# Two standard merge tiles fewer beside the first branch, one more pair by seven products, in an encoder trunk on Trainium2

## The chip, the cores and the metric

The kernel runs on one core of one Trainium2 chip. Its engines are TensorE (PE: matmuls, with PEld for weight loads), VectorE (DVE), ScalarE (ACT), GpSimd (POOL, hardly used here) and SyncE (SP, which only issues transfers here). ScalarE issues transfers too, from the same queue as its arithmetic (ACTq in the rows). The metric is device microseconds of one execution, the median of several runs.

## The reference

One layer of an encoder over 16 meta tokens, 512 prompt tokens and 256 sample tokens, with 2048 features, in float32. Normalised inputs are projected once, three mixers work on parts of the result, and sigmoid gates merge them:

```python
h = rmsnorm(z, norm_g)
cols = h @ w_in
u_a, gate_a, q_b, k_b, v_b, gate_b, glr_b, x_c, gate_c, merge = split_cols(cols)
y_a = s5_mixer(u_a, ...) * jax.nn.silu(gate_a)
y_b = gla_mixer(q_b, k_b, v_b, glr_b, ...) * jax.nn.silu(gate_b)
y_c = rglru_mixer(x_c, ...) * jax.nn.silu(gate_c)
gates = jax.nn.sigmoid(merge).reshape(bsz, length, N_BRANCH, D_MODEL)
m = (gates[:, :, 0] * (y_a @ w_out_a) + gates[:, :, 1] * (y_b @ w_out_b)
     + gates[:, :, 2] * (y_c @ w_out_c))
return z + m @ w_o
```

The `merge` part has 3 x 2048 columns: 48 tiles of 128 columns, each needed only near the end, when the branches are merged. They can be computed at any time after the input is normalised.

## The kernel before, in words

Each float32 product is made of three products of split halves (high x high, high x low, low x high), so one 128x128 weight block times 768 tokens is 6 matmuls of 384 columns.

**Two ways to a merge tile.** A standard tile (`merge_tile`, `fill_step`) goes over 16 blocks of features: 16 steps of 6 matmuls, 96 in all. The rest of the tiles are made in pairs in `strassen`, by seven products of half size in place of eight (`products`, `combine`): 168 matmuls for a pair. `NST` is the number of merge pairs made that way; 48 - 2 `NST` tiles are standard. With `NST` = 15 there are 18 standard tiles. Two are computed while the inputs are normalised, the other 16 are in the list `merges`. Every tile, made either way, is copied and spilled to memory (`gspill`).

**Standard tiles as cover.** The first branch (`branch_s5`) is mostly VectorE work with long chains. So that TensorE has something to do beside it, steps of standard tiles are put between its pieces. `Paced` wraps VectorE and adds up a charge for every operation. At each `tick` (line 287) a step (`fill_step`, matmuls at line 273) is written into the program for as long as the sum of charges is ahead of the steps' own clock, which advances by 1 / rate a step. The rate is the entry of `FILLS` for the stage, set by `pace`: 0 for the parameters, 1 for the chunk inputs, 2 for the scan over chunks (`advance`), 3 for the chunk outputs, 4 for gelu. Before stage 5 (the gating product, matmuls at line 728), and at each later call, `pace` also calls `flush`, which finishes an open tile. Stages 5 to 7 have rate 0. What is left in `merges` goes beside the end of the third branch (`cover(LT)`, 39 steps) and beside the first sums of `strassen`.

**The stages that the change touches.** In stage 3, for eight chunks e: `within(e + 2)` prepares coefficients (VectorE operations on `ca`, in three buffers; small products at line 634; `kt` copies on ScalarE; the store `kd` and the four loads `tp` on ScalarE's queue), then `chunk_out(e)` does 12 matmuls (lines 652 to 654), copies into `W`, and after chunks 3 and 7 stores `yd`. Stage 4 loads `fu` and `fy` on ScalarE's queue and computes gelu of four blocks (`fz`, `fh`, `fl`); stage 5 multiplies them by the gating weights. Then `branch_gla` begins: keys and queries are projected (matmuls at line 199, into the same four banks `psA` that the standard tiles use, two for each) and copied to `kk` and `qq`, then the values.

**What sets the order.** A planner at build time orders each engine's instructions: at each point the earliest in the program that it holds to be ready by its own costs. On the chip every engine then runs its list in that order. So work written later can stand earlier in an engine's list, and an instruction that waits holds up all behind it.

Of the kernel before, what the change touches and what calls it, by code (L numbers as in the profile page):

```python
# [19 lines left out]
HT = T // 2  # L20
HN = NT // 2
MAGIC = 12582912.0
FILLS = (0.2, 0.7, 1.6, 0.8, 1.1, 0, 0, 0)
SCRATCH = 1024
AHEAD = 6
SPLITN = 12
NST = 15
NA = 3
PREP = 6
WH = 3  # L30
# [65 lines left out]
def build(tc, A, out_p, out_s):  # L96
# [134 lines left out]

    merges = list(enumerate(MERGES[:48 - 2 * NST]))
    def merge_tile():
        i, (d, b) = merges.pop(0)
        merge_out(proj(MERGE0 + i, NM), d, b)
# [57 lines left out]
    def flush():  # L293

        fill["last"] = True
        while fill["k"] < 16 or fill["ws"]:
            fill_step()
        fill["last"] = False
# [86 lines left out]
    def pace(i):  # L385
        if i > 4:
            flush()
        fill.update(rate=FILLS[i], us=V.us)

# [1170 lines left out]
def strassen(E):  # L1560
# [52 lines left out]
    def weights(i, sb):  # L1613
        r = wp.tile([128, 4, 2, 128], F32, name="raw", bufs=2)
        SP.dma_start(r[:], A["w_st"][i, sb])
        rh = wp.tile([128, 3, 2, 128], F32R, name="hi")
        rl = wp.tile([128, 3, 2, 128], F32R, name="lo")
        split(rh[:], rl[:], r[:, 1:4])
        t = tp.tile([128, 4, 2, 128], F32, name="t")
        weight_sums(V, r, t)  # L1620
        th = wp.tile([128, 4, 2, 128], F32R, name="hi")
        tl = wp.tile([128, 4, 2, 128], F32R, name="lo")
        split(th[:], tl[:], t[:])
        return rh, rl, th, tl
# [14 lines left out]
    xp = tc.alloc_tile_pool(name="stu", bufs=1, reuse_waits="tile")  # L1639
    for i in range(NG2 + NST):  # L1640
        ps = {j: next_bank() for j in (1, 2, 3, 6, 7, 5, 4)}
        for sb in range(4):
            products(PE, ps, ahead.pop(0), sb, 8, operand)
            n = 4 * i + sb + 1
            if n > 2 and n < 4 * (NG2 + NST):
                ahead.append(weights(*divmod(n, 4)))
# [6 lines left out]
        if i < NG2:  # L1653
# [9 lines left out]
            continue  # L1663
        for g, (d, b) in zip((g1, g2), MERGES[48 - 2 * NST + 2 * (i - NG2):]):
            S.dma_start(E["gspill"][d, :, b, :], g[:])
# [29 lines left out]
def layout(inp):  # L1695
# [7 lines left out]
    order = [36 + 16 * b + d for d, b in MERGES]  # L1703
    std = order[:48 - 2 * NST]
    D["w_in"] = np.ascontiguousarray(w3[[i for i in range(36) if i not in GATES] + std])
    pairs = GATES + order[48 - 2 * NST:]
    st = []
# [88 lines left out]
```

## Time and profile before

| | us |
|---|---|
| median of three runs | 2037.04 |
| lowest and highest | 2035.94, 2038.36 |
| the profiled execution | 2038.42 |
| its span, first to last instruction | 2036.6 |

TensorE's granted clock was 0.996 of the full one in the mean. Engine idle time is read together with what ended it: an engine that is not the bottleneck may idle at no cost.

### The profile page before, as it was taken

The numbers are of one execution on the slowest core, as the hardware profiler recorded it, in microseconds if no ns is written. First come the engines' busy times: TensorE is split into PE (matmuls) and PEld (weight loads), VectorE is DVE, ScalarE is ACT, GpSimd is POOL, SyncE is SP. The second block draws the span as 40 slices with busy tenths as digits, with TensorE's granted clock in tenths as the row PEclk, the third lists the DMA queues.
The fourth block names the chain that finished last, engine by engine and source line by source line (L and its number), as shares of the span: only waits on it lengthen the run. The fifth ranks groups of instructions, "written<-read, shape, count | busy, mean of one in ns | idle before, by whom it ended". The sixth has DMA issues, their size and how long they took to land.

```text
span 2036.6 us, 30982 instructions
## 1 busy us (share of the span) xinstructions
PE 2003.8 (98%) x12228; PEld 1972.5 (97%) x12228; DVE 1504.9 (74%) x2784; ACT 808.2 (40%) x1172; POOL 0.2 (0%) x4
## 2 busy tenths in 40 slices
PE   8999999999999999999999999999999999999997
PEld 8999999999989999999999999999999999999997
DVE  8988983656567876977676656665669989887778
ACT  7332111443437675433333222222235435533345
POOL 0000000000000000000000000000000000000000
PEclk9999999999999999999999999999999999999999
DMA  8762234421111323543443222322355335532256
GB/s 292 251 123 94 75 102 120 147 80 49 61 52 45 102 72 122 179 133 102 139 135 112 94 94 100 103 91 100 104 183 215 125 114 180 176 117 94 94 163 218
DMA packets 105378, 252.12 MB, mean 124 GB/s; under 512 B 18960, under 2 KB 39952, under 8 KB 105232
## 3 DMA queue, kind: packets, MB, share of 16 engines
q1 hardware_dynamic: 77072, 200.61, 30.8%
q10 hardware_dynamic: 28160, 49.53, 6.9%
q8 instruction: 96, 1.57, 0.3%
q14 instruction: 50, 0.41, 0.1%
HBM read 200.65 MB, written 49.45 MB: 123 GB/s over the span
## 4 chain that ended last, share of the span: by engine, by line
PE 78%; DVE 13%; ACT 4%; DMA 3%; issue 1%; ACTq 0%; SPq 0%; DVEq 0%
PE pm L1149 24%; PE br L1149 23%; PE pm L199 10%; PE pm L273 5%; PE br L1422 4%; PE pm L1292 2%; PE br L1292 2%; DVE sc L61 2%; DVE W L61 2%; PE pm L332 2%; DVE lo L61 2%; ACT gt L89 1%; DMA c<-gspill 1%; DVE hb L61 1%; PE br L199 1%
## 5 line engine op out<-in xcount | busy, mean ns | idle before, releaser
L89 ACT ACTIVATE hi<-raw 128x768 fp32r<-128x768 f32 (+2 forms) x234 | 216.1, 924 | 482.8 <-PE br L1149 129.0
L61 DVE TENSOR_TENSOR lo<-raw,hi 128x768 fp32r<-128x768 f32 (+2 forms) x234 | 246.3, 1053 | 131.5 <-ACT hi L89 131.1
L61 DVE TENSOR_TENSOR lo<-t,hi 128x1024 fp32r<-128x1024 f32 x140 | 171.5, 1225 | 193.4 <-ACT hi L89 193.2
L89 ACT ACTIVATE hi<-t 128x1024 fp32r<-128x1024 f32 x140 | 148.4, 1060 | 279.6 <-PE pm L1149 138.3
L1149 PE MATMUL pm<-l,hi 128*128 128x384 f32 (+1 forms) x616 | 197.3, 320 | 0.0
L1149 PE MATMUL pm<-h,hi 128*128 128x384 f32 (+1 forms) x616 | 196.6, 319 | 0.2 <-ACT g L89 0.2
L1149 PE MATMUL pm<-h,lo 128*128 128x384 f32 (+1 forms) x616 | 196.6, 319 | 0.0
L1149 PE MATMUL br<-l,hi 128*128 128x384 f32 (+1 forms) x504 | 167.1, 331 | 0.0
L1149 PE MATMUL br<-h,hi 128*128 128x384 f32 (+1 forms) x504 | 165.9, 329 | 0.0
L1149 PE MATMUL br<-h,lo 128*128 128x384 f32 (+1 forms) x504 | 165.8, 329 | 0.0
L199 PE MATMUL pm<-h,hi 128*128 128x392 f32 (+1 forms) x608 | 161.8, 344 | 1.2 <-ACT xp L1022 1.2
L199 PE MATMUL pm<-h,lo 128*128 128x392 f32 (+1 forms) x608 | 159.5, 342 | 1.0 <-DVE lo L61 1.0
L199 PE MATMUL pm<-l,hi 128*128 128x392 f32 (+1 forms) x608 | 159.6, 341 | 0.0
L273 PE MATMUL pm<-h,lo 128*128 128x384 f32 x512 | 131.6, 338 | 2.5 <-DVE lo L61 2.5
L273 PE MATMUL pm<-h,hi 128*128 128x384 f32 x512 | 133.8, 342 | 0.0
L273 PE MATMUL pm<-l,hi 128*128 128x384 f32 x512 | 132.6, 340 | 0.0
L1149 PEld LDWEIGHTS pm<-h,hi 128*128 128x128 f32 x616 | 115.7, 188 | 0.7 <-ACT g L89 0.5
L1149 PEld LDWEIGHTS pm<-h,lo 128*128 128x128 f32 x616 | 116.0, 188 | 0.0
L1149 PEld LDWEIGHTS pm<-l,hi 128*128 128x128 f32 x616 | 115.7, 188 | 0.0
L199 PEld LDWEIGHTS pm<-h,hi 128*128 128x128 f32 x608 | 111.0, 188 | 2.7 <-ACT xp L1022 1.5
L199 PEld LDWEIGHTS pm<-h,lo 128*128 128x128 f32 x608 | 111.2, 188 | 1.5 <-DVE lo L61 1.3
L199 PEld LDWEIGHTS pm<-l,hi 128*128 128x128 f32 x608 | 110.6, 188 | 0.2
(358 smaller groups left out, 4799.6 us busy)
## 6 DMA issues: line engine op xcount, KB each, us to landing
raw<-in_w_st SPq DMA_DIRECT2D x92, 512.0 KB
raw<-in_w_in SPq DMA_DIRECT2D x74, 512.0 KB
gspill<-g ACTq DMA_DIRECT2D x48, 384.0 KB
raw<-in_w_ost SPq DMA_DIRECT2D x32, 512.0 KB
xr<-in_xT SPq DMA_DIRECT2D x31, 392.0 KB
m<-gspill SPq DMA_DIRECT2D x26, 384.0 KB
raw<-in_w_out SPq DMA_DIRECT2D x16, 512.0 KB
raw<-in_w_outc SPq DMA_DIRECT2D x16, 512.0 KB
```

Of the source, the lines that this page charges most:

```text
L61: return f(*a, **k)
L89: ins = self.eng.activation(**k)
L199: PE.matmul(ps[h][:, :nw], w[:, k, :], xx[kt][:, n0 + h * nw:n0 + (h + 1) * nw], start=(kt == 0 and j == 0), stop=(kt == 15 and j == 2))
L273: PE.matmul(ps[h][:, :HN], w[:, k % 8, :], xx[k][:, NM + h * HN:NM + (h + 1) * HN], start=(k == 0 and j == 0), stop=(k == 15 and j == 2))
L332: PE.matmul(ps0[2 * t + h][:, :HT], w[:, k, :], xx[kt][:, h * HT:(h + 1) * HT], start=(kt == 0 and j == 0), stop=(kt == 15 and j == 2))
L1149: PE.matmul(ps[j][:, :nt], w[:, wi, kk, :], x, start=(k == 0 and q == 0), stop=(k == n - 1 and q == 2))
L1292: PE.matmul(ps[h][:, :HN], w[:, 4 * b + k, :], yy[4 * b + k][:, h * HN:(h + 1) * HN], start=(k == 0 and j == 0), stop=(k == 3 and j == 2))
L1422: PE.matmul(po[:, :NS], x[:, n, :], y[k][:, ss], start=(first and j == 0), stop=(last and j == 2))
```

## The change

```diff
-FILLS = (0.2, 0.7, 1.6, 0.8, 1.1, 0, 0, 0)
+FILLS = (0.2, 0.7, 1.6, 0.15, 0.85, 0, 0, 0)
-NST = 15
+NST = 16
```

One more pair of merge tiles is made by seven products, so two fewer are standard; the rates of standard steps beside the chunk outputs (stage 3) and gelu (stage 4) are lower. The layout of the weights follows from `NST`; nothing else is edited.

## Rows read from the trace of the kernel before

**Rows 1.** The page's table of engines: busy us (share of the span), instructions.

```profile
PE 2003.8 (98%) x12228; PEld 1972.5 (97%) x12228; DVE 1504.9 (74%) x2784; ACT 808.2 (40%) x1172; POOL 0.2 (0%) x4
```

**Rows 2.** Busy time by stretch; the columns are in the first line.

```profile
core 0: us, PE busy (x) PEld busy (x) DVE busy (x) ACT busy (x) POOL busy (x), PEclk, DMA share, GB/s
285.00:382.00 97.00, 97.00 (x687) 93.78 (x686) 48.60 (x125) 21.44 (x42) 0.00 (x0) 1.00 0.47 143
382.00:415.00 33.00, 30.87 (x173) 29.51 (x172) 22.85 (x23) 15.84 (x23) 0.00 (x0) 1.00 0.41 130
415.00:456.00 41.00, 41.00 (x225) 39.80 (x224) 23.46 (x47) 15.67 (x29) 0.00 (x0) 1.00 0.19 65
900.00:1500.00 600.00, 600.00 (x3438) 600.00 (x3438) 393.06 (x602) 180.34 (x216) 0.00 (x0) 1.00 0.33 110
```

**Rows 3.** Groups of instructions: matmuls of standard steps (one of three groups).

```profile
L273 PE MATMUL pm<-h,lo 128*128 128x384 f32 x512 | 131.6, 338 | 2.5 <-DVE lo L61 2.5
```

**Rows 4.** Timeline of TensorE: start, length, line, tiles, count [idle before].

```profile
285.42 0.66 PE L634 MATMUL br<-ca,b 128*32 128x128 f32 x16
...
324.65 0.67 PE L634 MATMUL br<-ca,b 128*32 128x128 f32 x16
...
327.95 0.60 PE L273 MATMUL pm<-h,hi 128*128 128x384 f32 x2
...
342.73 0.35 PE L652 MATMUL br<-U,tp 128*128 128x96 f32 x2
...
381.76 0.52 PE L199 MATMUL pm<-h,lo 128*128 128x392 f32 x2
382.12 0.86 PE L728 MATMUL br<-fh,fwh 128*128 128x384 f32 x4
```

**Rows 5.** Timeline of ScalarE and its queue, 326 to 415 us.

```profile
326.25 2.47 ACTq L644 DMA_DIRECT2D tp<-kd  x4
...
342.76 0.49 ACT L89 ACTIVATE g<-pm 128x384 f32<-128x384 f32 x1 [12.08 <-PE pm L273]
342.94 0.60 ACTq L644 DMA_DIRECT2D tp<-kd  x1
...
364.92 0.87 ACT L89 ACTIVATE g<-pm 128x384 f32<-128x384 f32 x2 [14.08 <-PE pm L273]
...
366.69 0.48 ACTq L697 DMA_DIRECT2D fy<-yd  x1
...
414.78 0.89 ACT L89 ACTIVATE kk<-pm 128x392 f32<-128x392 f32 x2 [0.86 <-DVE fy L61]
```

**Rows 6.** Waits, 285 to 430 us: total, times, longest.

```profile
ACT g L89 <- PE pm L273: 26.2, 2, 14.1
...
DVE ca L61 <- PE br L653: 3.7, 3, 2.0
```

**Rows 7.** Timeline of ScalarE: copies of the first product, first and last of 23.

```profile
867.18 0.48 ACT L1163 COPY u<-br 128x384 f32<-128x384 f32 x1 [0.33 <-PE br L1149]
...
1512.61 0.46 ACT L1163 COPY u<-pm 128x384 f32<-128x384 f32 x1
```

**Rows 8.** TensorE around two idle places, and the clock by stretch.

```profile
268.94 0.62 PE L273 MATMUL pm<-h,lo 128*128 128x384 f32 x2 [2.04 <-DVE lo L61]
...
759.90 1.01 PE L1053 MATMUL br<-xch,gwh 128*128 128x402 f32 x4 [1.92 <-ACT xch L89]
...
269.40:272.80 3.40, 3.40 (x13) 3.40 (x13) 3.25 (x16) 0.65 (x1) 0.00 (x0) 0.53 0.42 154
273.00:276.40 3.40, 3.40 (x21) 3.40 (x21) 3.20 (x16) 0.97 (x3) 0.00 (x0) 1.00 0.29 116
761.00:764.00 3.00, 3.00 (x11) 2.97 (x10) 0.00 (x0) 1.82 (x4) 0.00 (x0) 0.52 0.00 0
```

**Rows 9.** Timeline of TensorE: end of the queries, end of the values.

```profile
418.47 0.51 PE L199 MATMUL pm<-h,lo 128*128 128x384 f32 x2
...
455.80 0.27 PE L822 MATMUL br<-ident,tmp 128*16 128x128 f32 x1
```

## Prediction

> **What bounds the kernel now.** I read the page's engine table first: TensorE is busy 98% of the span, VectorE 74%, ScalarE 40% [rows 1]. So time is TensorE work plus what TensorE waits. Then the table by stretch, for the stretches that the edit touches and the one where the added pair will lie: TensorE is full from 285 to 382 us, loses 2.1 us between 382 and 415, and is full again to 456 and over 900 to 1500 [rows 2]. VectorE is busy 49 of the 97 us up to 382. The order on TensorE comes next [rows 3, 4], then ScalarE's queue and its waits [rows 5, 6]: these tell how much later the first branch's own chain runs than it has to, because standard tile steps stand ahead of it.
>
> **What changes in the order.** One step of a standard tile is 6 matmuls, a tile 16 steps; the trace has 512 matmuls of each of the three operand kinds at L273, thus 1536 or 16 tiles [rows 3]. I count steps with the helper's own charges (0.065 us and 0.00104 us a column), which fix the order and are no times. A chunk's `within` is charged 5.0 us, six of them 30.0; at rate 0.8 this gives 25 steps (from the first tick on, so one more than the product), at 0.15 it gives 5. Gelu is charged 15.8: 18 steps at 1.1, 14 at 0.85. `flush` ends the open tile. Up to there 122 steps are unchanged, so before: 122 + 25 + 18 + 11 of the flush = 176 = 11 tiles; after: 122 + 5 + 14 + 3 = 144 = 9 tiles. With 14 tiles to place instead of 16, five are left for the third branch and the Strassen sums in both kernels, so nothing is moved there. The edit takes 32 steps away: 20 beside the chunk outputs, 12 beside gelu and its flush.
>
> **The part removed.** In the Strassen loop there are 23 copies of a pair's first product, the first at 867.18 and the last at 1512.61 us [rows 7]: 22 distances of 29.34 us, for 168 matmuls, 174.6 ns each. A standard step's matmuls keep that pace: 14 steps, 84 matmuls, fill the 14.78 us from 327.95 to 342.73 [rows 4], 176 ns each. Two tiles are 192 x 174.6 ns = **33.5 us** of TensorE. With them go four 512 KB loads on SP's queue and four splits (1.06 us on ScalarE and 1.22 us on VectorE each), which lie beside other work.
>
> **The part added.** One pair more: **29.3 us**, in a loop where TensorE is busy 600.00 of 600 us [rows 2]. Its four loads are of the same size and go on the same queue; its two spills replace the two tiles' spills on ScalarE's queue. VectorE has 393 us of work in 600 there [rows 2], about 19 us per 29.3, so its new splits and sums are covered; without cover it would be those 19 us. I put nothing on top.
> The Trainium skill, "TensorE: Matmul & The Clock Gate", section "Back-to-back issue gap", gives N/2.4 + 2.5 ns, for 384 columns an estimate of 162.5 ns. By it the tiles are 31.2, the pair 27.3 and the difference 3.9 us instead of 4.2. The measured pace decides.
>
> **What of the 33.5 us comes off the path.** If TensorE stayed full, all of it: 33.5 - 29.3 = 4.2 us faster. But where tiles were cover, their going shows the chain beneath. I follow it to the copy of the keys (`kk`) at 414.78 us, after which TensorE has its value projections to do up to 455.80 whatever came before [rows 5, 9]. The terms:
> - ScalarE stood 12.08 and 14.08 us in front of copies `g<-pm`, each waiting for the last step of a standard tile; behind the first stood the load of the last chunk's block (`tp`, 342.94), behind the second the loads that begin gelu (`fy`, 366.69) [rows 5]. That is 26.2 us in which the chain was merely queued [rows 6]. Fewer steps ahead of it give these back: 26.2.
> - The chunk loop: five rounds from 285.42 to 324.65, 7.85 us each [rows 4]. In a round VectorE builds `ca` anew once a chunk output has freed its buffer, and the next small products need it. VectorE waited 3.7 us for chunk outputs [rows 6]: all of it is given back if outputs run as soon as they can, nothing if the loop holds its order. Neither row is nearer, so the middle: 1.9.
> - Queries: their last matmul began at about 418.6, 4 us after `kk` could be copied [rows 5, 9]. With work pulled ahead they are done by then: 4.0, and 0 if not.
> - Against it: of a round's 7.85 us TensorE's own small products and chunk output take 3.3 (324.65 to 327.95 [rows 4]) and the one step left about 1.05, so it must find 3.5 us elsewhere. The planner does pull work forward: keys run at L199 ahead of the first matmul at L728, and 13 steps written for gelu ran between two chunk outputs [rows 4]. Where it fails there is a gap. After gaps of 2.04 and 1.92 us the granted clock was 0.53 and 0.52 in the stretch behind, the 1.2 GHz level. There 13 matmuls began in 3.4 us, at the full level 21: 8 x 0.175 = 1.4 us a time [rows 8]. I take one such drop; bounds 0 and five.
> The same page, in its section "Why this matters for your kernels", says that idle gaps throttle the array. The rows agree, and it speaks against thinning the cover.
>
> Sum: 26.2 + 1.9 + 4.0 - 1.4 = 30.7 us saved, 29.3 added: **1.4 us faster**. The profiled execution took 2038.42 (span 2036.6 and 1.8 around), so 2037.0 by it; it lies 1.38 above the median of the three runs, 2037.04. On the median's scale: **2035.6 us**.
>
> **Rivals.**
> - *Full cover.* The planner fills every gap with the 17 steps left, keys and queries. For it: they run ahead already, 16.8 us each. Against: four banks hold two projections, and no third can start before `kk` is copied. Time: 2037.04 - 4.2 = 2032.8; if the two idle places of 382 to 415 close too, 2030.8.
> - *Slower: the wrong place in the queue.* TensorE and ScalarE run in the planner's order. The `tp` loads of the seventh chunk were issued by 328.7, yet its output began at 342.73, behind a run of 14 steps [rows 4, 5]. If the planner puts 14 steps there again (the 17, or keys), the first 12.08 us are not given back, and these steps are then missing as cover beside gelu, where TensorE idles. Saved 30.7 - 12.1 = 18.6, net 10.7 slower: 2047.7; if half of it stays, 2041.7. It decides from less than 29.3 us saved.
> - *Slower: the clock.* Every round of the chunk loop leaves a gap long enough for the drop: four more at 1.4 us, 5.6 - 1.4 = 4.2 slower, 2041.2. Against: the small products keep TensorE occupied through much of a round, and the pulled work.
>
> **Chances.** Forecast (2033 to 2039.5) 0.50; full cover 0.26; wrong place 0.15; clock 0.09. A measurement of this kernel tells about 0.2%, 4.07 us, from no change. Full cover is just beyond it: faster 0.26. The forecast lies within it, with part of the clock's case: same 0.51. The rest is slower: 0.23. The range goes from the better end of full cover, 2031.0, to between the two sizes of the wrong place, 2043.5. The tail above holds about 0.1, the one below less.
>
> **What would show it.** Strassen copies still 29.3 us apart, the groups at L273 smaller by 64 (448). The `kk` copy between 384 and 392 us: at 389.5 or so the change breaks even, for 25.3 us earlier with the queries done (4.0) is 29.3. Waits of `g<-pm` for TensorE down from 26.2 to a few us. TensorE idle between 285 and 415 up by 2 to 5 us. Wrong if the seventh chunk output still stands behind a run of steps while gelu starts late, if the clock falls in several rounds, or if five tiles are not what is left.

## The result, and the profile after

The changed kernel took **2051.36 us** (median of 6 runs, 2050.20 to 2053.45), the kernel before 2037.13 on the same chip: ratio 1.007, 95% interval 1.0057 to 1.0083. It is 14.2 us slower, where I had forecast 1.4 faster and a range that ended at 2043.5. The profiled execution took 2050.43 (span 2048.0).

The engine table and the table by stretch of after, for the stretches of [rows 1, 2], and one of the three groups of standard steps [rows 3]:

```profile
PE 2004.7 (98%) x12204; PEld 1969.6 (96%) x12204; DVE 1515.1 (74%) x2807; ACT 808.6 (39%) x1173; POOL 0.2 (0%) x4
...
core 0: us, PE busy (x) PEld busy (x) DVE busy (x) ACT busy (x) POOL busy (x), PEclk, DMA share, GB/s
285.00:382.00 97.00, 92.05 (x622) 86.98 (x621) 57.64 (x136) 25.62 (x43) 0.00 (x0) 0.97 0.49 149
382.00:415.00 33.00, 27.04 (x130) 24.58 (x129) 20.61 (x36) 16.42 (x29) 0.00 (x0) 0.93 0.16 57
415.00:456.00 41.00, 40.85 (x232) 38.24 (x231) 21.99 (x50) 12.95 (x29) 0.00 (x0) 1.00 0.15 52
900.00:1500.00 600.00, 600.00 (x3438) 600.00 (x3437) 386.25 (x588) 177.16 (x208) 0.00 (x0) 1.00 0.32 106
...
L273 PE MATMUL pm<-h,lo 128*128 128x384 f32 x448 | 115.2, 338 | 4.1 <-DVE lo L61 4.1
```

TensorE does less (12204 matmuls for 12228), yet is busy 0.9 us longer: part of its work ran at half clock. Between 285 and 456 us it was idle 11.1 us, before 2.1. The Strassen loop is as full as before.

ScalarE's copies of a pair's first product, first and last of now 24 [rows 7]:

```profile
848.62 0.48 ACT L1163 COPY u<-br 128x384 f32<-128x384 f32 x1 [0.33 <-PE br L1149]
...
1523.38 0.46 ACT L1163 COPY u<-br 128x384 f32<-128x384 f32 x1
```

23 distances of 29.34 us. The loop begins 18.6 us earlier (of which 17.0 are there at the end of the values) and ends 10.8 us later: 18.6 gained, 29.3 paid. So the question is what became of the 33.5 us that two tiles cost. TensorE's timeline of after at the places of [rows 4, 8, 9]:

```profile
321.84 0.42 PE L273 MATMUL pm<-h,hi 128*128 128x384 f32 x1
...
330.15 0.51 PE L199 MATMUL pm<-h,hi 128*128 128x392 f32 x2
...
338.72 0.35 PE L652 MATMUL br<-U,tp 128*128 128x96 f32 x2
...
369.45 0.86 PE L728 MATMUL br<-fh,fwh 128*128 128x384 f32 x4
...
377.86 1.65 PE L728 MATMUL br<-fh,fwh 128*128 128x384 f32 x4 [3.53 <-ACT fh L89]
...
386.46 0.44 PE L728 MATMUL br<-fh,fwh 128*128 128x384 f32 x1 [1.44 <-ACT fwh L89]
...
388.76 0.44 PE L728 MATMUL br<-fh,fwl 128*128 128x384 f32 x1 [1.34 <-DVE fwl L61]
...
399.85 0.83 PE L199 MATMUL pm<-h,hi 128*128 128x392 f32 x2 [3.18 <-ACT kk L89]
...
438.80 0.27 PE L822 MATMUL br<-ident,tmp 128*16 128x128 f32 x1
```

First, 47 matmuls of standard steps (from 321.84) and 48 of a projection (330.15 to 338.72) stand between the sixth chunk's output and the seventh's, 16.9 us without a pause, where 14 steps had stood for 14.8 us. Then the rest of keys and queries runs, all of it before the gating matmuls begin at 369.45. From there TensorE has nothing but gating to do, and stops four times. ScalarE and its queue in the same stretch [rows 5]:

```profile
310.83 2.48 ACTq L644 DMA_DIRECT2D tp<-kd  x4
313.35 6.14 ACTq L660 DMA_DIRECT2D yd<-W  x7
319.54 0.27 ACT L637 COPY kt<-br 128x128 f32<-128x128 f32 x1 [12.43 <-DMA yd<-W]
...
330.17 0.49 ACT L89 ACTIVATE g<-pm 128x384 f32<-128x384 f32 x1 [7.60 <-PE pm L273]
330.41 0.60 ACTq L644 DMA_DIRECT2D tp<-kd  x1
...
331.05 4.36 ACTq L644 DMA_DIRECT2D tp<-kd  x7
...
352.89 0.44 ACTq L697 DMA_DIRECT2D fy<-yd  x1
...
383.89 1.99 ACT L89 ACTIVATE ft<-br,small 128x384 f32<-128x384 f32 x4 [2.64 <-PE br L728]
...
399.30 0.89 ACT L89 ACTIVATE kk<-pm 128x392 f32<-128x392 f32 x2 [0.71 <-DVE fy L61]
```

and the waits of after, 285 to 430 us [rows 6] (total, times, longest):

```profile
ACT kt L637 <- DMA yd<-W: 12.4, 1, 12.4
ACT kt L637 <- DMA tp<-kd: 10.7, 2, 6.1
...
ACT g L89 <- PE pm L273: 7.6, 1, 7.6
```

The hold for standard tiles is down from 26.2 to 7.6, as forecast. But the 7.6 that are left stand in front of the `tp` loads of the seventh and of the last chunk (issued from 330.41 to 335.41), where the 12.08 of before stood in front of the last one's alone. And another hold has grown: the copy `kt` for the seventh chunk stands behind eight stores of chunk outputs to `yd` (L660) that ScalarE issues itself. The last seven take it 0.88 us each here, and the copy starts 0.05 us after them. The trace of before had that wait too, in a row that I did not use:

```profile
317.52 4.11 ACTq L660 DMA_DIRECT2D yd<-W  x7
321.67 0.27 ACT L637 COPY kt<-br 128x128 f32<-128x128 f32 x1 [8.71 <-DMA yd<-W]
```

**Where the 33.5 us went.** Of these, 17.0 arrived at L822. Additional idle time from 285 to 456 us is 8.9. Two stretches after stops ran at the half level of the clock (first and third row; columns as in the table by stretch):

```profile
376.60:383.40 6.80, 5.54 (x16) 5.02 (x17) 4.63 (x6) 2.85 (x4) 0.00 (x0) 0.50 0.32 96
384.00:387.00 3.00, 1.56 (x9) 1.24 (x9) 2.02 (x2) 2.41 (x5) 0.00 (x0) 1.00 0.00 0
400.50:403.90 3.40, 3.40 (x11) 3.08 (x11) 2.42 (x5) 0.45 (x2) 0.00 (x0) 0.51 0.07 26
```

At granted clocks of 0.50 and 0.51, 5.54 and 3.40 us of work lost 4.4 us. A stop of 2.0 us from 277.5 (a `lo` split on VectorE), where before stopped for 0.46, adds 1.5. 17.0 + 8.9 + 4.4 + 1.5 = 31.8; 1.7 us I can't assign.

### The profile page after: what moved, and what is told of

Read it like the earlier page. It is cut to its first block, busy times and chain, and to the rows that moved or that the text cites. A ratio compares the mean times of both kernels' runs of the same rounds, so it can differ in the third digit from the quotient of the medians.

```text
span 2048.0 us, 30986 instructions
## 1 busy us (share of the span) xinstructions
PE 2004.7 (98%) x12204; PEld 1969.6 (96%) x12204; DVE 1515.1 (74%) x2807; ACT 808.6 (39%) x1173; POOL 0.2 (0%) x4
## 4 chain that ended last, share of the span: by engine, by line
PE 78%; DVE 13%; ACT 4%; DMA 4%; issue 1%; ACTq 0%; SPq 0%; DVEq 0%
PE br L1149 24%; PE pm L1149 23%; PE pm L199 10%; PE pm L273 3%; PE pm L1422 3%; PE br L1292 2%; PE pm L1292 2%; DVE sc L61 2%; DVE W L61 2%; DVE lo L61 2%; PE pm L332 2%; PE br L1422 1%; DMA x<-xnorm 1%; ACT gt L89 1%; DVE hb L61 1%
## 5 line engine op out<-in xcount | busy, mean ns | idle before, releaser
L1149 PE MATMUL br<-l,hi 128*128 128x384 f32 (+1 forms) x576 | 187.6, 326 | 0.0
L1149 PE MATMUL pm<-l,hi 128*128 128x384 f32 (+1 forms) x576 | 187.5, 326 | 0.0
L1149 PE MATMUL br<-h,lo 128*128 128x384 f32 (+1 forms) x576 | 186.7, 324 | 0.1
L1149 PE MATMUL pm<-h,lo 128*128 128x384 f32 (+1 forms) x576 | 186.6, 324 | 0.0
L1149 PE MATMUL br<-h,hi 128*128 128x384 f32 (+1 forms) x576 | 186.4, 324 | 0.0
L273 PE MATMUL pm<-h,lo 128*128 128x384 f32 x448 | 115.2, 338 | 4.1 <-DVE lo L61 4.1
L273 PE MATMUL pm<-h,hi 128*128 128x384 f32 x448 | 117.2, 342 | 0.0
L273 PE MATMUL pm<-l,hi 128*128 128x384 f32 x448 | 116.1, 340 | 0.0
L199 PEld LDWEIGHTS pm<-l,hi 128*128 128x128 f32 x608 | 111.0, 188 | 0.2
L1149 PEld LDWEIGHTS br<-h,lo 128*128 128x128 f32 x576 | 108.5, 188 | 0.4 <-DVE lo L61 0.4
```

The costliest lines, as they stand in the source:

```text
L199: PE.matmul(ps[h][:, :nw], w[:, k, :], xx[kt][:, n0 + h * nw:n0 + (h + 1) * nw], start=(kt == 0 and j == 0), stop=(kt == 15 and j == 2))
L273: PE.matmul(ps[h][:, :HN], w[:, k % 8, :], xx[k][:, NM + h * HN:NM + (h + 1) * HN], start=(k == 0 and j == 0), stop=(k == 15 and j == 2))
L1149: PE.matmul(ps[j][:, :nt], w[:, wi, kk, :], x, start=(k == 0 and q == 0), stop=(k == n - 1 and q == 2))
```

## Experiments

Three theories. **The list**: the chain of the first branch is held by ScalarE's own list: the `yd` stores stand in front of the work of the last chunks, and taking standard steps away leaves that hold. **Cover**: the lower rates are at fault (too few steps as cover, and with them the clock), whatever the queues do. **Price**: the pair itself costs more than 29.3 us. (Where an expectation below says "theory A" or "rival", it spells out beside it which one it means in that run.) Marks, in us, of all kernels (the sixth and the last chunk: start of the last matmul of its output; the ratio is to the kernel before as it was measured beside each):

| kernel | sixth chunk | last chunk | `kk` copy | first L822 | first L1163 copy | time | ratio (95%) |
|---|---|---|---|---|---|---|---|
| before | 327.9 | 350.0 | 414.8 | 455.8 | 867.2 | 2037.1 | 1 |
| after | 321.8 | 343.9 | 399.3 | 438.8 | 848.6 | 2051.4 | 1.0057–1.0083 |
| e1 rates alone | 325.6 | 347.8 | 403.4 | 442.8 | 884.7 | 2054.0 | 1.0065–1.0095 |
| e2 pair alone | 327.0 | 349.2 | 413.4 | 454.4 | 855.4 | 2058.5 | 1.0089–1.0119 |
| e3 after, 16 stores on SyncE | 319.4 | 330.2 | 390.1 | 431.0 | 842.0 | 2046.4 | 1.0027–1.0055 |
| e4 before, same | 327.5 | 335.1 | 418.7 | 471.7 | 881.2 | 2057.2 | 1.0079–1.0109 |
| e5 after, 8 stores on SyncE | 319.5 | 330.2 | 392.2 | 431.7 | 840.9 | 2046.5 | 1.0033–1.006 |
| e6 before, same | 327.4 | 335.5 | 401.5 | 454.5 | 864.3 | 2037.0 | 0.9987–1.0005 |
| e7 more cover beside chunks | 326.3 | 349.5 | 411.3 | 450.8 | 857.4 | 2058.3 | one run |
| e8 cover beside gelu only | 320.9 | 344.8 | 399.8 | 439.2 | 849.6 | 2054.4 | one run |
| e9 = e5 + held queries | 319.7 | 330.7 | 390.4 | 428.0 | 838.2 | 2040.9 | 1.0003–1.0021 |
| e10 after + held queries | 325.0 | 347.1 | 402.0 | 439.6 | 850.3 | 2051.7 | 1.0053–1.008 |
| e11 pair, lower `LT` | 327.2 | 349.4 | 413.9 | 454.9 | 859.5 | 2060.7 | 1.01–1.0127 |

The marks are those of the one profiled execution of each, the times are medians. In e5 and e3 that execution was the shortest (2041.39 and 2043.44). And up to the sixth chunk e1 and e10 have the work of after, yet reach it at 325.6 and 325.0 and not at 321.8: in both TensorE's clock was at 0.50 for over 6 us in the chunk loop. So single marks differ by up to 4 us for that reason alone.

### The two halves of the change

e1 is the kernel before with the rates of after:

```diff
-FILLS = (0.2, 0.7, 1.6, 0.8, 1.1, 0, 0, 0)
+FILLS = (0.2, 0.7, 1.6, 0.15, 0.85, 0, 0, 0)
```

> The lower rates alone, still 15 pairs: nine standard tiles beside the first branch, and the two that are left over go beside the third branch's end and the Strassen sums. If the first branch gave back only 17.0 of the 33.5 us in the changed kernel because its own chain is bare there, and TensorE is full where the two tiles go, the time is 2037.1 + 16.5 = 2053.6 us. Rival: the sums are short of cover and take the tiles for less than their 33.5 us: 2040 to 2048.

e2 is the kernel before with the pair alone:

```diff
-NST = 15
+NST = 16
```

> One pair more at the old rates: the first branch keeps eleven tiles, so two fewer are left for the third branch's end and the Strassen sums (three instead of five). If the pair's price is 29.3 us and those places need no cover, 2037.1 - 4.2 = 2032.9 us. If the sums are a chain of their own that the tiles cover (41 steps before, 9 here), up to all of the 33.5 us stays: 2037 to 2066. The keys' copy stands at 414.8 us as in the kernel before, by either.

e1 took 2053.99 us, 16.0 more than the kernel before beside it (2037.97) and as expected (2053.6), though it computes the very same tiles in the same way: they are only placed later, some 20 steps of them after 840 us, ahead of the Strassen loop. So the loss comes from the place, and the price theory falls: the loss is there without the pair, and the pair costs 29.34 us in the loop. (The medians of e1 and after lie 2.6 us apart, which their intervals don't tell from nothing.) With the old rates the pair makes it worse still, 2058.47, inside the second range of its expectation. TensorE's timeline of e2, at its largest stop:

```profile
832.12 0.69 PE L1149 MATMUL br<-sh,hi 128*128 128x384 f32 x1 [24.00 <-ACT hi L89]
```

The two tiles are then missing beside the sums of the Strassen operands: TensorE waits 24.0 us for ScalarE, and from 832 to 836 us, behind the stop, the granted clock is 0.50. So the standard steps are cover in both places. That fits the count in the prediction: with five tiles left for the third branch and the sums, that part of after is as full as before's.

e11 tries whether the third branch can spare them (fewer steps there, so that more are left for the sums):

```diff
-LT = 39
+LT = 15
```

> The kernel before with the one pair more (NST 16) and its own rates, and the charge of steps beside the third branch's last part lowered from 39 to 15, so that the sums of the Strassen loop's operands keep 33 standard steps beside them instead of 9. The run e2_pair_alone had lost 24.0 us of TensorE there. Theory A (the two tiles can be missed beside the third branch but not beside the sums): the 24 us gap at 808 us is gone, the stretch up to 458 us is as in before, time 2033 to 2037. Rival (the steps were cover beside the third branch too): TensorE idles there by about as much as it gains, time 2045 to 2060.

TensorE of e11, three of its stops:

```profile
787.67 1.01 PE L273 MATMUL pm<-h,hi 128*128 128x384 f32 x2 [2.99 <-ACT hi L89]
...
793.56 1.01 PE L273 MATMUL pm<-h,lo 128*128 128x384 f32 x2 [4.24 <-DVE lo L61]
...
835.60 0.69 PE L1149 MATMUL br<-sh,hi 128*128 128x384 f32 x1 [14.36 <-ACT hi L89]
```

It took 2060.68 us: the expectation of theory A is missed. The time is 0.7 us above the rival's range, but not by its mechanism: the third branch's own matmuls show no new stop; the one in the sums went from 24.0 to 14.4 us, and TensorE waited 7.2 us for the weights of standard steps at 787 and 793 us. The lower charge moved only two steps before 770 us. Whether the third branch can spare a tile stays open.

### How many steps, and where

e7 puts the steps beside the chunk outputs (`FILLS` 0.7 and 0 there and beside gelu), e8 beside gelu only (0 and 0.85), both with the pair:

```diff
-FILLS = (0.2, 0.7, 1.6, 0.15, 0.85, 0, 0, 0)
+FILLS = (0.2, 0.7, 1.6, 0.7, 0, 0, 0, 0)     # e7
+FILLS = (0.2, 0.7, 1.6, 0, 0.85, 0, 0, 0)    # e8
```

> The changed kernel with the same nine standard tiles, but all 22 steps left placed beside the chunk outputs (rates 0.7 and 0). If the chain of the first branch sets the time, the keys' copy stands within 4 us of the changed kernel's 399.3, whatever place the steps have. If it is the place of the cover, more of it beside the chunk outputs holds the last chunk back, the keys' copy comes at 403 or later: 2055 us or more.

> The same nine tiles with no step beside the chunk outputs and 22 beside gelu and its flush (rates 0 and 0.85). Chain: the keys' copy within 4 us of 399.3, 2047 to 2055 us. Place of the cover: fewer steps in front of the last chunks, the keys' copy at 395 or earlier, 2046 us or less.

e8 had `kk` at the same place as after (399.8), within the range of its first expectation. Its last chunk still comes 23.9 us behind the sixth, in before and after 22.1. ScalarE and TensorE in e8:

```profile
312.48 4.15 ACTq L660 DMA_DIRECT2D yd<-W  x7
316.67 0.27 ACT L637 COPY kt<-br 128x128 f32<-128x128 f32 x1 [9.34 <-DMA yd<-W]
...
322.48 5.00 ACTq L644 DMA_DIRECT2D tp<-kd  x8
```

```profile
331.01 0.51 PE L199 MATMUL pm<-h,hi 128*128 128x392 f32 x2
...
339.59 0.36 PE L652 MATMUL br<-U,tp 128*128 128x96 f32 x2
```

The hold at the stores is there again, but it is not what the seventh chunk waits for last: all eight `tp` loads are issued by 327.5, and two chunks earlier an output began 2.1 us after its loads were issued. The seventh output begins at 339.59, behind 57 matmuls of steps and 48 of a projection that run without a pause. No step is charged to the chunk outputs here; the planner pulled steps written for gelu into the place, and keys behind them. So in e8 TensorE's order holds the last chunks.

e7 had `kk` 12.0 us later than after, as its second expectation said, but it is no test of the place alone: its trace has 160 steps ahead of the third branch, ten tiles and not the nine that were expected, so it carries one tile (16.8 us of matmuls) more there. With 64 steps left where after has 80, TensorE stopped 11.7 us in the sums. Each of the two has one time only, so the marks are what is read here.

### The stores on ScalarE's queue

e3 is the kernel after, e4 the kernel before, with all 16 stores of the last two blocks issued by SyncE:

```diff
-                S.dma_start(ydv[j, :, gs], W[j * 16:(j + 1) * 16, gs, 97:193])
+                SP.dma_start(ydv[j, :, gs], W[j * 16:(j + 1) * 16, gs, 97:193])
```

> The changed kernel with the sixteen stores of the chunk outputs (yd) issued from SyncE's queue and not from ScalarE's. Theory A (ScalarE's queue: its stores, loads and waiting copies stand in the first branch's chain, 12.4 us of them in front of the seventh chunk's kt copy): the last chunk output ends 6 to 12 us earlier, the keys' copy too, and the time falls to 2039 to 2045 us. Theory B (the chain is long by latencies and by gelu itself, wherever its transfers are issued): the keys' copy moves by under 3 us, 2048 to 2052 us.

> The kernel before with the same stores on SyncE's queue. Both theories: TensorE is full there, so within 2 us of 2037.1 us. A gain of over 4 us would say that the kernel before is held by that queue too.

In e3 the last chunk follows the sixth by 10.8 us instead of 22.1, and L822 comes 7.8 us earlier than in after: that speaks for the list. The time, 2046.38, is 1.4 us above theory A's range. SyncE's queue also carries loads. ScalarE in e3, and SyncE's queue and TensorE in e4:

```profile
349.01 0.63 ACT L89 ACTIVATE fwh<-fw 128x512 fp32r<-128x512 f32 x1 [12.40 <-DMA fw<-in_w_glu]
```

```profile
313.44 38.79 SPq L660 DMA_DIRECT2D yd<-W  x16
```

```profile
379.52 1.33 PE L728 MATMUL br<-fh,fwh 128*128 128x384 f32 x3 [14.87 <-ACT fh L89]
```

In e4 the stores occupy that queue for 38.8 us (the last eight follow the last chunk's output), and the weight loads behind them are issued only from 352 us on. TensorE's list has no projection between the standard steps and gating there, and it stops for 14.9 us until gelu's first results (`fh`). I had expected no change from e4 and it lost 0.94%: a miss. It fits the list theory on another queue; how much of the stop is the queue and how much the planner's order is not separated.

So e5 (after) and e6 (before) move only the eight stores of the first of the two blocks:

```diff
-                S.dma_start(ydv[j, :, gs], W[j * 16:(j + 1) * 16, gs, 97:193])
+                (SP if e == 3 else S).dma_start(ydv[j, :, gs], W[j * 16:(j + 1) * 16, gs, 97:193])
```

> The changed kernel with only the first eight stores of the chunk outputs (after the fourth chunk) on SyncE's queue; the last eight stay on ScalarE's. Theory A (those eight issues stand in front of the seventh chunk's kt copy, and the sixteen on SyncE held up the loads of the gating weights): the last chunk output ends near 330 us as with all sixteen moved, gelu's first square comes before 345 (349.6 there), the keys' copy stands at 383 to 387, under the 389.5 us at which the change breaks even, and the time is 2031 to 2036 us. Theory B (gelu and the gating product are long by themselves): the keys' copy stays at 390 or later and the time is 2042 to 2047 us.

> The kernel before with the same eight stores on SyncE's queue. TensorE is full there in either theory: within 3 us of 2037.5 us, if SyncE's loads of the standard tiles' weights are not held up by them; 2050 or more if they are, as with all sixteen.

ScalarE in e5:

```profile
314.54 0.27 ACT L637 COPY kt<-br 128x128 f32<-128x128 f32 x1 [2.09 <-DMA tp<-kd]
...
320.63 0.27 ACT L637 COPY kt<-br 128x128 f32<-128x128 f32 x1 [5.68 <-DMA tp<-kd]
...
363.22 1.06 ACT L89 ACTIVATE hi<-raw 128x1024 fp32r<-128x1024 f32 x1 [4.31 <-DMA raw<-in_w_in]
...
376.79 1.99 ACT L89 ACTIVATE ft<-br,small 128x384 f32<-128x384 f32 x4 [6.17 <-PE br L728]
```

The wait for stores is gone, sixth to last chunk is 10.7 us, and e5 is 4.9 us faster than after. But the edit changed more than that wait. TensorE at the seventh output of e5:

```profile
321.99 0.36 PE L652 MATMUL br<-U,tp 128*128 128x96 f32 x2
```

Only 9 matmuls of steps stand between the sixth and this one, where after has 47 and 48 of a projection: with the stores elsewhere the planner made another order. So e5 and e3 show that the place of the eight stores decides when the last two chunks come. They don't tell the wait on the chip from the planner's order, and e8 speaks for the order.

The numbers miss: I expected 2031 to 2036 and got 2046.49. 24.1 us saved at L822 are 5.2 less than 29.3, which accounts for the profiled execution (2041.39) and not for the rest of the median's 9.2. The 13.7 us gained at the last chunk shrink to 7.1 at `kk` and stay so (7.1) at L822. ScalarE now waits elsewhere: for a weight load whose split stands in front of gelu's next activation (4.31), and for the gating matmuls (6.17), which TensorE begins only after three quarters of keys and queries (144 of 192 matmuls).

e6 is the control that tells most. The same edit makes `kk` 13.3 us earlier in the kernel before, and L822 1.3 us earlier, the time unchanged. Where TensorE is full, a shorter chain is worth nothing; in after it is worth 7.1.

### TensorE's order ahead of gating

e9 is e5, e10 is after, each with the second half (48 matmuls) of the first queries' projection made to follow the gating matmuls of block 1 in TensorE's order:

```diff
+        if m == 1:
+            E["glu"] = mm            # last matmul of L728 in block 1
...
-        evac(t[:], proj(8 + hp, NM), NM, scale=0.125)
+        evac(t[:], proj(8 + hp, NM, None if hp else E["glu"]), NM, scale=0.125)
```

> The kernel after with two edits: the eight stores of chunk 3's block of yd on SyncE's queue instead of ScalarE's (as in the run e5_after_half), and the second half (48 matmuls) of the first queries' projection made to follow the last gating matmul at L728 of block m=1 in TensorE's order. Theory A (what is left of the loss in e5_after_half is order: TensorE runs keys and queries ahead of the gating matmuls, so that ScalarE's first sigmoid waits 6.2 us for L728, and gating then has nothing beside it): first sigmoid at about 370 us instead of 377, copy of the keys at about 386 instead of 392, first matmul at L822 at 423 to 428 instead of 432, time 2033 to 2041. Rival (gelu's own chain on ScalarE and VectorE and its load fix the keys' copy, whatever TensorE's order): copy of the keys unchanged at about 392, idle TensorE time moved only, time about 2046.

> The kernel after with the hold of the run e9_half_hold alone (second half of the first queries' projection behind the gating matmuls of block m=1), all stores of yd on ScalarE's queue as in after. Theory A: the seventh chunk still waits behind ScalarE's stores (its output ends at about 344 as in after), the gating part loses less: 3 to 5 us at L822, time 2046 to 2049. Rival (order of TensorE does not matter there): 2051 within 2 us.

ScalarE in e9 (its lines are 3 to 5 higher: L728 is L731), and TensorE's table of the stretch in e5 and then in e9:

```profile
373.64 2.00 ACT L89 ACTIVATE ft<-br,small 128x384 f32<-128x384 f32 x4 [2.56 <-PE br L731]
...
390.43 0.87 ACT L89 ACTIVATE kk<-pm 128x392 f32<-128x392 f32 x2
```

```profile
350.00:393.00 43.00, 37.38 (x211) 36.39 (x209) 27.29 (x30) 19.69 (x28) 0.00 (x0) 1.00 0.39 126
```

```profile
350.00:391.00 41.00, 37.68 (x214) 36.72 (x212) 27.33 (x29) 20.22 (x28) 0.00 (x0) 1.00 0.41 137
```

The first sigmoid comes 3.2 us earlier than in e5, the idle time of the stretch falls from 5.6 to 3.3 us (and the mean clock of 370 to 405 us rises from 0.95 to 1.00), L822 begins at 428.0, and the kernel takes 2040.93 us. L822 and the time are where theory A had put them (the time just inside, at the end of the range); `kk` at 390.4 and the sigmoid at 373.6 are later than its 386 and 370. 27.8 us saved and 29.3 added would be 1.5 us; e9 is 0.03 to 0.21% (0.6 to 4.3 us) slower than the kernel before, so the sum holds. In e10 the time is no better than after's (2051.73, as the rival said), and its last chunk still comes 22.1 us behind the sixth, at 347.1. But that the order behind it does not matter is not shown: its profiled execution lost over 3 us to the clock in the chunk loop, and from the last chunk to L822 it takes 92.5 us where after takes 94.9.

No kernel here beat the one before.

## Why the prediction was wrong, step by step

- **Steps and counts: right.** 448 matmuls in each group at L273, thus 14 tiles; five tiles after the first branch in both.
- **The part added: right.** 29.3 us predicted, 29.34 measured, TensorE still full in the loop.
- **"Fewer steps ahead of it give these back: 26.2": the step that failed.** 7.7 came back. Of the 12.08 us ahead of the last two chunks nothing did: sixth to last chunk takes 22.1 us in both kernels. Of the 14.08 ahead of `fy` 7.7 came back (last chunk's output to its load's issue 16.7 before, 9.0 after). I took one row of the waits [rows 6] as if nothing else stood in that place and nothing would come into it. TensorE's list was filled again there (95 matmuls, 16.9 us, between the sixth and the seventh output; before 84 and 14.8), 7.6 us of the tile hold stayed, in front of the loads of both last chunks, and the wait of `kt` behind the stores, 8.7 us in before and in the same view, became 12.4. e5 shows the stores as a cause: with these eight elsewhere 9 matmuls stand in that place and the 22.1 us are 10.7. Whether by the wait itself or by the order that the planner makes on account of it stays open. A hold that goes returns only the difference to the next one.
- **The chunk loop, 1.9 (0 to 3.7): too small.** The sixth chunk came 6.1 us earlier, 1.8 of it already at the first chunk.
- **Gelu and gating, put at nothing:** from `fy`'s load to `kk` 48.1 us before and 46.4 after, 1.7 gained. With the terms above, 6.1 + 0 + 7.7 + 1.7 = 15.5 us, the whole gain at `kk`.
- **Queries, 4.0: 1.5 arrived.** They were done by `kk`, as foreseen; but TensorE stopped 3.2 us for `kk` and then worked 3.4 us at a clock of 0.51.
- **The clock, one drop of 1.4: too small.** Two drops in this stretch, 4.4 us. Not in the chunk loop, where I looked for them (its rival fails in this trace: a stop of 1.17 us there left the clock at 1.00; in e1 and e10 the clock did fall there once), but beside gating.
- **That work would be pulled forward was foreseen; where it would then be missing was not counted.** I wrote that the planner pulls keys and queries forward to fill gaps, and took that as help. It is the same work that had covered gating: pulled forward, it left TensorE idle 6.0 us from 382 to 415. e9 puts a quarter of it back and gains 3.6 us at L822.
- **The rivals.** "The wrong place in the queue" came nearest: 48 matmuls of the keys stand ahead of the seventh chunk again, the first 12.1 us are not given back, 18.6 us saved by its sum against 17.0 at L822 and 18.6 at the first Strassen copy, 2047.7 against 2051.4. I gave it 0.15. Its mechanism is what the traces of after and e8 show on TensorE; what it did not have is that the place of ScalarE's stores goes with it (e5). Full cover fell with the idle time. The break-even rule (29.3 us saved) held for e9, which with 27.8 at L822 is at 1.0012; the median of e5 is 4 us above it.
- **The last 2.2 us** between 12.0 (profiled executions) and 14.2 (medians) is where the two profiled executions lie in their own runs: 1.3 above the median in before, 0.9 below in after.

The Trainium skill, "Perfetto Trace Analysis", section "What "DMA-bound" means", says that an engine's track of solid DMA slices is the making of descriptors, not the moving of data. The trace has such a stretch: seven stores fill 6.14 us of ScalarE's list and the copy behind starts 0.05 us later. That these 6.14 us are the making of descriptors, no run here shows. The Trainium skill, "TensorE: Matmul & The Clock Gate", section "Why this matters for your kernels", says that idle gaps between bursts of matmuls make the throughput drop. The trace agrees for the stops of 3.53 and 3.18 us (0.50 and 0.51 behind), and for 1.44 and 1.34 us it shows 1.00.

## What to carry to other kernels

When a wait is to be taken away, list all that the same engine's list holds between the two ends of that chain, its DMA issues too: what comes back is the difference to the next wait, not the length of the one removed. Ask also what the scheduler will put into the place that comes free. Work that a scheduler pulls forward to fill one gap is missing where it stood; count cover over the whole stretch up to the next point where TensorE is full by itself, and test by an edit that only shortens the chain (e6) whether the chain or TensorE's work sets the end there. A queue with loads on it is no free place for stores that wait (e4).

## What the runs showed that I had not expected

- Issuing a 96 KB store with short rows cost ScalarE 0.51 us at the median and up to 1.47; seven in a row took 4.11 us in before and 6.14 in after, for as many bytes.
- Whether a stop of TensorE was followed by the half clock differed at the same place: at the small products in the third round of the chunk loop a stop of 1.17 us (after) and of 1.41 (e9) left it at 1.00; one of 1.52 (e10) was followed by 6.8 us at 0.50, one of 1.88 (e1) by some 6 us (TensorE's timeline and the table by stretch of e10):

```profile
296.99 0.38 PE L637 MATMUL br<-ca,b 128*32 128x128 f32 x2 [1.52 <-DVE b L61]
```

```profile
298.60:305.40 6.80, 6.80 (x38) 6.23 (x38) 3.63 (x11) 2.70 (x6) 0.00 (x0) 0.50 0.23 67
```

- The length of a stop does not settle it either. At 268.9 us, where both kernels run the same list, before stopped for 2.04 us and went on at 0.53 [rows 8]; after stopped for 2.07 and went on at 1.00. The half level came in after behind its next stop, of 2.00 us at 279.51 (0.51 from 281.0 to 284.4), and in e3 two stops of 2.04 and 2.00 us at these places were followed by 1.00 each time. After:

```profile
268.83 0.62 PE L273 MATMUL pm<-h,lo 128*128 128x384 f32 x2 [2.07 <-DVE lo L61]
```

```profile
269.40:272.80 3.40, 3.40 (x22) 3.40 (x21) 3.25 (x15) 0.65 (x1) 0.00 (x0) 1.00 0.46 154
```
